# Loading the tokens by two queues, and taking the first norm's sums of squares from token-major tiles

## The chip, the cores and the metric

The kernel runs on one core of one Trainium2 chip. The core has five engines that run side by side, each in its own instruction order: TensorE (PE, with its weight loads shown apart as PEld), VectorE (DVE), ScalarE (ACT), GpSimd (POOL) and SyncE (SP). SP and ACT also issue DMA transfers; an issue is an instruction in their order like any other. The metric is the device time of one execution in microseconds (us). The kernel before takes 1518.39 us, the median of three runs (1518.27 to 1519.29).

## The reference

Two pre-norm residual layers over 512 tokens of width 1024, then a final RMSNorm. What matters for the change is the head of the first layer:

```
h = rms_norm(x, norm1_g[l])          # y = x * rsqrt(mean(x*x) + EPS); y * g
z = h @ w_in[l]
(u_ssm, dq, dk, dv, iq, ik, iw, rq, rk, rv, rg, gates) = split_cols(z)
ya = s5_mixer(u_ssm, ...)
yb = dsa_mixer(rope(dq), rope(dk), dv, rope(iq), rope(ik), iw)
yc = retention_mixer(rope(rq), rope(rk), rv, rg, ...)
x = x + (g_a*(ya @ w_proj_a) + g_b*(yb @ w_proj_b) + g_c*(yc @ w_proj_c)) @ w_out[l]
x = x + square(relu(rms_norm(x, norm2_g[l]) @ w_ff1[l])) @ w_ff2[l]
```

The factor rsqrt(mean(x*x) + EPS) is one number for each token. Scaling by it can be done after the product with w_in, and the kernel does so.

## The kernel before, in words

The tokens arrive token-major: eight tiles `xt` of 128 tokens x 512 channels (256 KB each), four token blocks t for each half hf of the channels. PE transposes them in groups of four into a PSUM bank `tr` of 128 channels x 512 tokens; there are eight such groups m. From each bank ACT writes `xgh` (the tokens times the gain g1, rounded to float32r), DVE writes the remainder `xgl`, DVE copies the bank to the residual page `x`, and ACT squares it (`sq`) while DVE adds the square to one page `ssq`. Each float32 product is made of three float32r products: high x high, high x low, low x high. A weight tile is loaded as `raw` by SP, cast to `wh` on ACT, and its remainder `wl` is made on DVE; three buffers of each go round.

`Norm.stats` turns `ssq` into one factor for each token. Four products with a column of ones (`stat`) sum over the partitions, DVE forms mean + EPS (`st_v`), POOL raises it to the power -0.5 (`st_r`), DVE puts the four blocks on diagonals (`sq<-ct,st_r`), PE spreads them over all partitions (`statb`), and ACT copies the result out (`rbc`).

After the tokens, layer 0 goes on with the product for keys, values and indexer (`mm`, 292 columns, `tm_group(l, C_DK, ...)`), whose four banks ACT moves out as `z<-mm,st_r`, scaled by `st_r`; with the product for the state-space branch (`mx`, two blocks of 512 tokens), which DVE scales by `rbc` into `s5u` and ACT and POOL shuffle in 32 small copies into `u`; and with the query product (`mm`, 384 columns, `C_DQ`). Its four PSUM banks are those of the 292-column product, so it starts when the first `z` is out. Then come products for gates (`mm`, 512 columns), which fill PE while DVE, ACT and POOL prepare the state-space and attention branches.

The order of each engine is not written by hand: a scheduler orders the instructions at build time from priorities (weight loads are taken early) and from its own model of the time. At run time each engine keeps its order and waits on semaphores. DMAs use eight semaphores in turn (DMAHW0 to DMAHW7); an issue also waits until the transfer that used its semaphore last has landed.

All calls go through one helper, so the profile puts nearly everything on line 110; instructions are told apart by the names of their tiles.

Of the kernel before, what the change touches and what calls it, by code (L numbers as in the profile page):

```python
# [12 lines left out]
AF = mybir.ActivationFunctionType  # L13
ALU = mybir.AluOpType

P = 128
SEQ = 512
DM = 1024
DEPTH = 2
KB = DM // P  # L20
NT = SEQ // P
EPS = 1e-6
# [71 lines left out]
def build(tc, x, positions, norm1_g, w_in, lam_re, lam_im, log_step, b_re, b_im, c_re, c_im, ssm_d,  # L94
# [5 lines left out]
    class Ordered:  # L100


        def __init__(self, e):
            self._e = e
# [16 lines left out]
    pe, ve, sc, gp, sy = (Ordered(e) for e in (nc.tensor, nc.vector, nc.scalar, nc.gpsimd, nc.sync))  # L121
    es = contextlib.ExitStack()
    with es:
# [4 lines left out]
        def f(t):  # L128
            return t.bitcast(F32)

        def page(dtype=F32, name="pg", tag="pg"):
            t = pool.tile([P, 512], dtype, tag=tag, bufs=BUFS[tag], name=name)
            pending[t.tensor.name] = tag
            return t

        def tpage(dtype=F32, name="ta"):
            return page(dtype, name, "ta")
# [7 lines left out]
        def small(n, name, bufs=2, dtype=F32):  # L145
            return pool.tile([P, n], dtype, tag=name, bufs=bufs, name=name)
# [4 lines left out]
        def mx_ps(name="mx"):  # L151
            return psp.tile([P, 512], F32, tag="mx", bufs=4, name=name)

        def copy(o, i, scale=1.0):
            sc.activation(o, i, AF.Copy, scale=scale)
# [4 lines left out]
        def stt(o, a, s, b, op0, op1):  # L160
            ve.scalar_tensor_tensor(o, a, s, b, op0=op0, op1=op1)

        ct = cp.tile([P, CONSTS.shape[1]], F32, name="ct")
        xt = {}
        rows = [spage(name="rows"), spage(name="rows")]
        with tc.high_priority():
            sc.dma_start(out=ct[:, :P], in_=consts[:, :P])
            sc.dma_start(out=rows[0][:DEPTH * KB, :P], in_=norm1_g.rearrange("l (k p) -> (l k) p", p=P))
            for hf in range(2):
                for t in range(NT):  # L170
                    z = tpage(name="xt")
                    sy.dma_start(out=z, in_=x[0, t * P:(t + 1) * P, hf * 512:(hf + 1) * 512])
                    xt[hf, t] = z

        def cst(n):
# [4 lines left out]
        ones = cp.tile([P, P], F32, name="ones")  # L180
# [10 lines left out]
        g1 = cp.tile([P, DEPTH * KB], F32, name="g1")  # L191
# [8 lines left out]
        def more_consts():  # L200
            z = rows[1]
            gp.memset(z[:, :P], 0.0)
            for name, src in (("g2", norm2_g.rearrange("l (k p) -> (l k) p", p=P)),
                              ("rg", ret_g.rearrange("l (k p) -> (l k) p", p=P)),
                              ("gb", glu_b.rearrange("l (k p) -> (l k) p", p=P)),
                              ("lr", lam_re.rearrange("l (i a) p -> (l i) (a p)", a=2)),
                              ("li", lam_im.rearrange("l (i a) p -> (l i) (a p)", a=2))):
                o, n = R_OFF[name], src.shape[0]
                sy.dma_start(out=z[o:o + n, :P], in_=src)
            o = R_OFF["sd"]  # L210
            sy.dma_start(out=z[o:o + 8 * DEPTH, 96:P], in_=ssm_d.rearrange("l (i a) c -> (l i) (a c)", a=2))
            q = z[96:96 + 8 * DEPTH]
            sy.dma_start(out=q[:, P:P + 2], in_=log_step.rearrange("l (i a) -> (l i) a", a=2))
            ve.tensor_copy(q[:, :P].rearrange("p (a s) -> p a s", s=64), q[:, P:P + 2, None].to_broadcast([8 * DEPTH, 2, 64]))
            ps = columns(z, 96 + 8 * DEPTH)
            ve.tensor_copy(vec[:, :N_ROWS], ps[:, :N_ROWS])
            ve.tensor_copy(vec[:, N_ROWS:], ps[:, 96:96 + 8 * DEPTH])
            glb2 = cp.tile([P, DEPTH * 2], F32, name="glb2")
            ve.tensor_scalar(glb2, vec[:, R_OFF["gb"]:R_OFF["gb"] + 2 * DEPTH], 0.5, None, op0=ALU.mult)
            sy.dma_start(out=ct[:, P:], in_=consts[:, P:])  # L220
            return glb2
# [68 lines left out]

        class Norm:
            def __init__(self):
                self.h, self.l, self.acc = [None] * KB, [None] * KB, None

            def feed(self, m, gcol, src=None, cc=slice(0, SEQ), room=None):
                src = xp[m][:, cc] if src is None else src
                if gcol is not None:
                    h, lo = (page(F32R, n, "xg") if room is None else room() for n in ("xgh", "xgl"))
                    copy(h, src, gcol)
                    stt(lo, src, gcol, f(h), ALU.mult, ALU.subtract)  # L300
                    self.h[m], self.l[m] = h, lo
                if self.acc is None:
                    self.acc = page(name="ssq", tag="ssq")
                if m == 0:
                    sc.activation(self.acc[:, cc], src, AF.Square)
                else:
                    s = page(name="sq", tag="sq")
                    sc.activation(s[:, cc], src, AF.Square)
                    ve.tensor_tensor(self.acc[:, cc], self.acc[:, cc], s[:, cc], ALU.add)

            def pair7(self, k, gc, ngc, room):
# [11 lines left out]
                for src, h, lo in ((t1, ah, al), (t2, ch, cl)):  # L323
# [4 lines left out]
                return [(z[:, q], y[:, q]) for z, y, q in ((oh, ol, ha), (eh, el, ha), (eh, el, hz), (ch, cl, hz),  # L328
                                                          (ah, al, ha), (ch, cl, ha), (ah, al, hz))]

            def stats(self, bc=True, ts=range(NT)):
                ps = mx_ps("stat")
                for t in ts:
                    pe.matmul(ps[:, 2 * t:2 * t + 2], self.acc[:, t * P:(t + 1) * P], ones[:, 0:2], start=True, stop=True)
                v = small(NT, "st_v")
                tt = slice(ts[0], ts[-1] + 1)
                ve.tensor_scalar(v[:, tt], ps[:, 0:2 * NT].rearrange("p (t a) -> p t a", a=2)[:, tt, 0], 1.0 / DM, EPS,
                                 op0=ALU.mult, op1=ALU.add)
                r = small(NT, "st_r")
                gp.tensor_tensor(r[:, tt], v[:, tt], nhalf[:, tt], ALU.pow)  # L340
                if not bc:
                    return r, None
                dg = page(name="sq", tag="sq")
                for t in range(NT):
                    ve.tensor_scalar(dg[:, t * P:(t + 1) * P], ident, r[:, t:t + 1], None, op0=ALU.mult)
                pb = mx_ps("statb")
                pe.matmul(pb, ones, dg, start=True, stop=True)
                rb = page(name="rbc", tag="rbc")
                copy(rb, pb)
                return r, rb  # L350
# [379 lines left out]
        def tr4(blocks, psf=None):  # L730

            ps = (psf or mx_ps)("tr")
            for t, b in enumerate(blocks):
                w = b.shape[-1]
                pe.transpose(ps[:w, t * P:(t + 1) * P], b, ident)
            return ps
# [514 lines left out]
        nrm = Norm()  # L1251
        for m in range(KB):
            if m == 4:
                glb2 = more_consts()
            ps = tr4([xt[m // 4, t][:, (m % 4) * P:(m % 4 + 1) * P] for t in range(NT)])
            nrm.feed(m, g1[:, m:m + 1], ps)
            xp[m] = page(name="x%d" % m)
            mark.append(ve.tensor_copy(xp[m], ps).ins.name)
        o5 = None
        for l in range(DEPTH):  # L1260
            nrm, o5 = layer(l, nrm, o5)
# [22 lines left out]
```

## Time and profile before

| what | value |
|---|---|
| median of three runs | 1518.39 us |
| the profiled execution | 1518.57 us, span 1516.8 us |
| PE, PEld busy | 97%, 85% of the span |
| DVE, ACT, POOL busy | 81%, 46%, 4% |
| DMA, mean | 95 GB/s |
| TensorE clock granted, by slices of 38 us | under 0.9 of full only in the second (38 to 76 us) |

The span is from the first to the last recorded instruction; the profiled execution is 1.8 us longer. A line of a timeline gives start, duration, engine, operation, tile written <- tiles read, shape, and in brackets how long the engine had been idle before it and what released it. Start to start, not the duration, is what a matmul costs in a row of matmuls, because they overlap.

### The profile page before, as it was taken

How to read it: one execution, taken by the hardware profiler on the slowest of the kernel's cores; microseconds unless marked ns; L12 is line 12 of the kernel's file. 1: busy time of each engine (PE TensorE's matmuls, PEld its weight loads, DVE VectorE, ACT ScalarE, POOL GpSimd, SP SyncE). 2: the span in 40 equal slices, each digit the busy share in tenths (PEclk: the TensorE clock that was granted, in tenths of full speed). 3: DMA queues.
4: the chain of work that ended last, by engine and by line, in shares of the span. 5: the costliest groups of instructions: out<-in, count | busy, mean ns of one | idle time of the engine just before them, and what ended most of it. 6: DMA issues, size and time to landing. Idle time of an engine off the chain costs nothing.

```text
span 1516.8 us, 22081 instructions
## 1 busy us (share of the span) xinstructions
PE 1468.6 (97%) x8202; PEld 1288.4 (85%) x8202; DVE 1224.0 (81%) x2618; ACT 696.2 (46%) x1154; POOL 59.3 (4%) x131
## 2 busy tenths in 40 slices
PE   5999999999998999999999999999999999999997
PEld 5888988877887998889888889988778888998887
DVE  7876899985899878987775769998568888777876
ACT  5654653453534443344455743344445434343343
POOL 0211100000010000100001100000000000000000
PEclk9899999999999999999999999999999999999999
DMA  6221222323322333233342223322143323333343
GB/s 221 77 81 42 81 70 73 94 70 101 108 63 91 111 98 99 83 108 95 119 130 76 84 57 94 94 70 84 56 153 90 95 93 98 111 98 102 94 126 111
DMA packets 138993, 144.17 MB, mean 95 GB/s; under 512 B 11835, under 2 KB 131461, under 8 KB 138885
## 3 DMA queue, kind: packets, MB, share of 16 engines
q1 hardware_dynamic: 138132, 141.63, 31.0%
q8 instruction: 64, 1.05, 0.3%
q10 hardware_dynamic: 752, 1.12, 0.2%
q14 instruction: 45, 0.36, 0.1%
HBM read 136.44 MB, written 6.29 MB: 94 GB/s over the span
## 4 chain that ended last, share of the span: by engine, by line
PE 83%; DVE 10%; ACT 4%; issue 2%; DMA 1%; POOL 0%; SPq 0%; POOLq 0%; DVEq 0%; ACTq 0%
PE mm L110 58%; PE f L110 17%; DVE wl L110 2%; ACT u L110 1%; PE mx L110 1%; PE pv L110 1%; PE sp L110 1%; PE ry L110 1%; PE tr L110 1%; DVE zr L110 1%; DVE ang L110 1%; PE pt L110 1%; ACT s5f L110 1%; DVE x L110 1%; PE s5y L110 1%
## 5 line engine op out<-in xcount | busy, mean ns | idle before, releaser
L110 ACT ACTIVATE wh<-raw 128x1024 fp32r<-128x1024 f32 (+4 forms) x318 | 310.4, 978 | 528.6 <-PE mm L110 287.7
L110 DVE TENSOR_TENSOR wl<-raw,wh 128x1024 fp32r<-128x1024 f32 (+4 forms) x318 | 355.2, 1118 | 120.0 <-ACT wh L110 116.7
L110 PE MATMUL f<-xc,wh 128*128 128x256 f32 x1344 | 242.8, 281 | 0.0
L110 PE MATMUL mm<-sql,wh 128*128 128x512 f32 (+1 forms) x544 | 207.2, 382 | 1.3 <-DVE sql L110 1.2
L110 PE MATMUL mm<-sqh,wh 128*128 128x512 f32 (+1 forms) x544 | 207.0, 382 | 1.3 <-DVE fft L110 1.1
L110 PE MATMUL mm<-sqh,wl 128*128 128x512 f32 (+1 forms) x544 | 206.1, 381 | 0.0
L110 PEld LDWEIGHTS f<-xc,wh 128*128 128x128 f32 x1344 | 205.4, 188 | 0.0
L110 PE MATMUL f<-xc,wl 128*128 128x256 f32 x644 | 174.6, 281 | 1.3 <-DVE wl L110 1.3
L110 PE MATMUL mm<-xgh,wh 128*128 128x512 f32 x384 | 152.3, 397 | 0.0
L110 PE MATMUL mm<-xgh,wl 128*128 128x512 f32 x384 | 152.1, 397 | 0.0
L110 PE MATMUL mm<-xgl,wh 128*128 128x512 f32 x384 | 151.9, 396 | 0.0
L110 DVE TENSOR_TENSOR raw<-raw 128x256 f32<-128x256 f32 (+1 forms) x336 | 107.3, 330 | 30.0 <-DMA raw<-in_w_ff_dram 27.8
L110 PEld LDWEIGHTS mm<-sql,wh 128*128 128x128 f32 x544 | 102.3, 188 | 21.6 <-DVE sql L110 1.9
L110 PEld LDWEIGHTS mm<-sqh,wh 128*128 128x128 f32 x544 | 102.2, 188 | 21.7 <-issue 1.5
L110 PEld LDWEIGHTS f<-xc,wl 128*128 128x128 f32 x644 | 118.7, 188 | 1.9 <-DVE wl L110 1.5
L110 PEld LDWEIGHTS mm<-sqh,wl 128*128 128x128 f32 x544 | 102.4, 188 | 21.0
L110 PE MATMUL mm<-wl,xgh 128*128 128x384 f32 (+1 forms) x320 | 107.5, 338 | 1.7 <-DVE wl L110 1.7
L110 PE MATMUL mm<-wh,xgh 128*128 128x384 f32 (+1 forms) x320 | 103.5, 340 | 4.6 <-ACT z L110 2.8
L110 PE MATMUL mm<-wh,xgl 128*128 128x384 f32 (+1 forms) x320 | 104.5, 338 | 0.0
L110 DVE TENSOR_TENSOR x<-x,mm 128x512 f32<-128x512 f32 (+1 forms) x136 | 88.3, 650 | 12.9 <-PE mm L110 12.6
L110 PEld LDWEIGHTS mm<-xgh,wl 128*128 128x128 f32 x384 | 72.3, 188 | 16.1
L110 PEld LDWEIGHTS mm<-xgl,wh 128*128 128x128 f32 x384 | 72.3, 188 | 15.5
(383 smaller groups left out, 2676.9 us busy)
## 6 DMA issues: line engine op xcount, KB each, us to landing
raw<-in_w_ff_dram SPq DMA_DIRECT2D x76, 512.0 KB, 3.5
raw<-in_w_ff_dram SPq DMA_DIRECT2D x112, 256.0 KB, 2.8
raw<-in_w_in_dram SPq DMA_DIRECT2D x52, 512.0 KB, 3.6
raw<-in_w_in_dram SPq DMA_DIRECT2D x32, 384.0 KB, 3.3
raw<-in_w_out_dram SPq DMA_DIRECT2D x16, 512.0 KB, 3.4
xd<-x SPq DMA_DIRECT2D x16, 256.0 KB, 2.2
x<-xd SPq DMA_DIRECT2D x16, 256.0 KB, 5.6
raw<-in_w_proj_c_dram SPq DMA_DIRECT2D x8, 384.0 KB, 3.2
```

What stands on the lines that cost most here:

```text
L110: r = fn(*a, **k)
```

## The change

Two edits. First, the four token tiles of the second half (hf = 1) are issued by ACT's queue and not by SP's. Second, in the first norm of layer 0 alone, the squares are no longer taken from the transposed banks and added up on DVE. A new function `token_sums` squares each token-major tile on ACT as it stands in SBUF, with the sum over its 512 channels as a by-product of the instruction (`accum_out`); a DVE addition of four columns joins the two halves. `stats` then skips the four `stat` products. The later norms are as before.

```diff
-                    sy.dma_start(out=z, in_=x[0, t * P:(t + 1) * P, hf * 512:(hf + 1) * 512])
+                    (sc if hf else sy).dma_start(out=z, in_=x[0, t * P:(t + 1) * P, hf * 512:(hf + 1) * 512])
...
-            def feed(self, m, gcol, src=None, cc=slice(0, SEQ), room=None):
+            def feed(self, m, gcol, src=None, cc=slice(0, SEQ), room=None, squares=True):
...
+                if not squares:
+                    return
...
+            def token_sums(self, xt):
+
+                q = small(2 * NT, "st_q", 1)
+                for (hf, t), z in xt.items():
+                    s = page(name="sq", tag="sq")
+                    sc.activation(s, z, AF.Square, accum_out=q[:, hf * NT + t:hf * NT + t + 1])
+                self.sums = small(NT, "st_s", 1)
+                ve.tensor_tensor(self.sums, q[:, :NT], q[:, NT:], ALU.add)
+
             def stats(self, bc=True, ts=range(NT)):
-                ps = mx_ps("stat")
-                for t in ts:
-                    pe.matmul(ps[:, 2 * t:2 * t + 2], self.acc[:, t * P:(t + 1) * P], ones[:, 0:2], start=True, stop=True)
                 v = small(NT, "st_v")
                 tt = slice(ts[0], ts[-1] + 1)
...
+                if self.sums is None:
+                    ps = mx_ps("stat")
+                    for t in ts:
+                        pe.matmul(ps[:, 2 * t:2 * t + 2], self.acc[:, t * P:(t + 1) * P], ones[:, 0:2], start=True, stop=True)
+                    sums = ps[:, 0:2 * NT].rearrange("p (t a) -> p t a", a=2)[:, tt, 0]
+                else:
+                    sums = self.sums[:, tt]
+                ve.tensor_scalar(v[:, tt], sums, 1.0 / DM, EPS, op0=ALU.mult, op1=ALU.add)
...
-            nrm.feed(m, g1[:, m:m + 1], ps)
+            nrm.feed(m, g1[:, m:m + 1], ps, squares=False)
...
+        nrm.token_sums(xt)
```

The scheduler orders the first layer's mixer anew; from its end on the orders of all engines are the same. On ACT at the head of the program, from the third weight cast on, stood before:

```order
L110 ACTIVATE wh<-raw 128x584 [waits DMAHW4_49]
L110 ACTIVATE xgh<-tr,g_89 128x512 [waits DVE_49,PE_49]
L110 ACTIVATE xgh<-tr,g_89 128x512 [waits PE_49] x2
L110 ACTIVATE ssq<-tr 128x512 [waits DVE_49]
L110 ACTIVATE xgh<-tr,g_89 128x512 [waits PE_49]
```

and stands now:

```order
L110 ACTIVATE wh<-raw 128x584 [waits DMAHW4_49]
L110 DMA xt<-in_x_dram 128x512 x2
L110 DMA xt<-in_x_dram 128x512 [waits DMAHW6_49]
L110 DMA xt<-in_x_dram 128x512 [waits DMAHW0_49]
L110 ACTIVATE sq,st_q<-xt 128x512 [waits DMAHW5_49]
L110 ACTIVATE sq,st_q<-xt 128x512
L110 ACTIVATE xgh<-tr,g_89 128x512 [waits DVE_49,PE_49]
L110 ACTIVATE sq,st_q<-xt 128x512 [waits DMAHW7_49,Activation_49]
L110 ACTIVATE sq,st_q<-xt 128x512 [waits DMAHW1_49,Activation_49]
L110 ACTIVATE xgh<-tr,g_89 128x512 [waits PE_49]
```

Four issues and two squares have come in front of the first `xgh`, and two more squares between the first and the second. The fourth issue waits for DMAHW0, the semaphore of the fourth `raw` tile.

On PE at the end of the 292-column product stood before (the last rows of that product, `stat`, and the first of the query product):

```order
L110 MATMUL mm<-wh,xgl 128x292 [waits DVE_49]
L110 MATMUL mm<-wh,xgl 128x292 x3
L110 MATMUL stat<-ones,ssq 128x2 [waits DVE_49,PE_49]
L110 MATMUL stat<-ones,ssq 128x2 x3
L110 MATMUL mm<-wh,xgh 128x384 [waits Activation_49]
L110 MATMUL mm<-wl,xgh 128x384
```

Now `statb` and the first products of the state-space branch stand inside the 292-column product, in its sixth and seventh groups of twelve:

```order
L110 MATMUL statb<-sq,ones 128x512 [waits DVE_49,PE_49]
L110 MATMUL mm<-wh,xgl 128x292 [waits DVE_49]
L110 MATMUL mm<-wh,xgl 128x292 x3
L110 MATMUL mm<-wh,xgh 128x292 [waits Activation_49]
L110 MATMUL mm<-wl,xgh 128x292
L110 MATMUL mm<-wh,xgh 128x292
L110 MATMUL mm<-wl,xgh 128x292
L110 MATMUL mm<-wh,xgh 128x292
L110 MATMUL mm<-wl,xgh 128x292
L110 MATMUL mm<-wh,xgh 128x292
L110 MATMUL mm<-wl,xgh 128x292
L110 MATMUL mx<-xgh,wh 128x512 [waits DVE_49,PE_49]
```

What moved: `stat` is gone, and the query product, which followed it, now comes after all 48 products `mx`, none of which waits for the factors.

On ACT after the shuffles of the state-space input (`u`, 24 of the 32 copies) stood before, up to the cast of the query product's fourth and last weight tile:

```order
L110 ACTIVATE u<-s5u 32x128 x11
L110 ACTIVATE kt<-tr 128x512 [waits PE_49] x2
L110 ACTIVATE vhl<-z_501 128x4x64
L110 ACTIVATE ikt<-tr 128x512 [waits PE_49]
L110 ACTIVATE iqs<-z_501 128x4x32 [waits DMAHW7_49]
L110 ACTIVATE iqs<-z_501 128x4x32 x3
L110 ACTIVATE iqs<-z_501 128x4x32 [waits DMAHW3_49]
L110 ACTIVATE iqs<-z_501 128x4x32
L110 ACTIVATE wh<-raw 128x768 [waits DMAHW4_49,PE_49]
```

and stands now:

```order
L110 ACTIVATE u<-s5u 32x128 x11
L110 ACTIVATE iks<-z_492 128x4x32 [waits DVE_49]
L110 ACTIVATE iks<-z_492 128x4x32
L110 ACTIVATE kt<-tr 128x512 [waits PE_49] x2
L110 ACTIVATE vhl<-z_492 128x4x64
L110 ACTIVATE wh<-raw 128x768 [waits DMAHW4_49,PE_49]
```

The cast has moved ahead of `ikt` and the six `iqs`.

## Rows read from the trace of the kernel before

**Rows 1.** Waits of PE, 0 to 100 us: total, times, longest.

```profile
PE stat L110 <- DVE ssq L110: 4.0, 1, 4.0
PE mm L110 <- ACT z L110: 2.8, 1, 2.8
PE mm L110 <- DVE wl L110: 1.7, 1, 1.7
PE mm L110 <- ACT wh L110: 1.6, 1, 1.6
```

**Rows 2.** Chain that ended last, 0 to 110 us: start, duration.

```profile
34.38 1.06 POOL st_r L110
...
68.36 16.90 PE mm L110 x65
```

**Rows 3.** Timeline of PE and its weight loads, 8 to 75 us.

```profile
11.43 0.72 PEld L110 LDWEIGHTS tr<-ct,xt 128*128 128x128 f32 x4 [0.41 <-DMA xt<-in_x_dram]
...
32.20 1.02 PE L110 MATMUL stat<-ones,ssq 128*128 128x2 f32 x8 [4.04 <-DVE ssq L110]
36.01 0.69 PE L110 MATMUL mm<-wh,xgh 128*128 128x384 f32 x1 [2.79 <-ACT z L110]
...
40.02 1.05 PE L110 MATMUL statb<-sq,ones 128*128 128x512 f32 x2
...
54.42 0.34 PE L110 MATMUL mm<-wh,xgh 128*128 128x384 f32 x1
54.60 0.34 PE L110 MATMUL mm<-wl,xgh 128*128 128x384 f32 x1
...
65.72 0.97 PE L110 MATMUL mm<-wh,xgh 128*128 128x384 f32 x4 [1.63 <-ACT wh L110]
...
70.12 0.52 PE L110 MATMUL mm<-wh,xgl 128*128 128x384 f32 x1
70.44 0.52 PE L110 MATMUL mm<-wl,xgh 128*128 128x384 f32 x1
```

**Rows 4.** Busy time in stretches: PE, PEld, DVE, ACT, POOL, granted clock, DMA share, GB/s.

```profile
10.00:15.00 5.00, 4.85 (x28) 4.05 (x27) 2.33 (x4) 3.06 (x6) 0.00 (x0) 1.00 1.02 345
...
35.00:40.00 5.00, 3.99 (x12) 3.99 (x13) 5.00 (x46) 2.74 (x8) 0.42 (x1) 0.50 0.00 1
...
65.00:70.00 5.00, 2.62 (x9) 2.30 (x10) 5.00 (x14) 2.56 (x3) 0.00 (x0) 0.74 0.11 14
70.00:75.00 5.00, 5.00 (x19) 4.96 (x18) 4.97 (x15) 1.94 (x4) 0.00 (x0) 0.58 0.88 275
```

**Rows 5.** The same view, longer stretches.

```profile
160.00:200.00 40.00, 36.30 (x210) 33.83 (x210) 34.53 (x102) 26.21 (x60) 3.49 (x11) 0.96 0.26 76
200.00:330.00 130.00, 130.00 (x651) 111.63 (x650) 125.41 (x311) 52.94 (x100) 4.67 (x4) 1.00 0.27 80
```

**Rows 6.** Timeline of ACT, 0 to 70 us.

```profile
0.73 0.44 ACTq L110 DMA_DIRECT2D ct<-in_consts_dram  x1
...
7.89 0.69 ACT L110 ACTIVATE wh<-raw 128x584 fp32r<-128x584 f32 x1 [2.03 <-DMA raw<-in_w_in_dram]
11.95 1.84 ACT L110 ACTIVATE xgh<-tr,g 128x512 fp32r<-128x512 f32 x3 [3.37 <-PE tr L110]
...
50.20 5.29 ACT L110 ACTIVATE u<-s5u 32x128 f32<-32x128 f32 x12 [2.90 <-DVE s5u L110]
...
64.84 2.72 ACT L110 ACTIVATE wh<-raw 128x768 fp32r<-128x768 f32 x3
```

**Rows 7.** Groups by form, ACT, 0 to 260 us: count, busy us, mean ns, idle before.

```profile
L110 ACT ACTIVATE sq<-tr 128x512 f32<-128x512 f32 x7 | 4.0, 608 | 1.8 <-DVE ssq L110 1.8
...
L110 ACT ACTIVATION_READ_ACCUMULATOR sm<-sm,at_nm 128x1 f32 x6 | 1.1, 187 | 0.0
```

**Rows 8.** Groups by form, DVE, 0 to 40 us.

```profile
L110 DVE TENSOR_TENSOR ssq<-ssq,sq 128x512 f32<-128x512 f32 x7 | 4.8, 681 | 0.0
```

**Rows 9.** Waits of DVE, 0 to 200 us.

```profile
DVE wl L110 <- ACT wh L110: 19.5, 10, 5.4
```

More of the change, by code (lines that the diff above doesn't have):

```diff
@@ L292, in __init__ @@
             def __init__(self):
-                self.h, self.l, self.acc = [None] * KB, [None] * KB, None
-            def feed(self, m, gcol, src=None, cc=slice(0, SEQ), room=None):
+                self.h, self.l, self.acc, self.sums = [None] * KB, [None] * KB, None, None
+            def feed(self, m, gcol, src=None, cc=slice(0, SEQ), room=None, squares=True):
                 src = xp[m][:, cc] if src is None else src
@@ L329, in pair7 @@
                                                           (ah, al, ha), (ch, cl, ha), (ah, al, hz))]
+            def token_sums(self, xt):
[5 more added lines that the diff above has]
+                ve.tensor_tensor(self.sums, q[:, :NT], q[:, NT:], ALU.add)
             def stats(self, bc=True, ts=range(NT)):
-                ps = mx_ps("stat")
-                for t in ts:
-                    pe.matmul(ps[:, 2 * t:2 * t + 2], self.acc[:, t * P:(t + 1) * P], ones[:, 0:2], start=True, stop=True)
                 v = small(NT, "st_v")
                 tt = slice(ts[0], ts[-1] + 1)
-                ve.tensor_scalar(v[:, tt], ps[:, 0:2 * NT].rearrange("p (t a) -> p t a", a=2)[:, tt, 0], 1.0 / DM, EPS,
-                                 op0=ALU.mult, op1=ALU.add)
+                if self.sums is None:
[6 more added lines that the diff above has]
+                ve.tensor_scalar(v[:, tt], sums, 1.0 / DM, EPS, op0=ALU.mult, op1=ALU.add)
                 r = small(NT, "st_r")
```

## The prediction

> **What bounds the kernel now.** I read the page first: PE is busy for nearly the whole span, so the question is where it is not, and what ends the wait there. The waits of PE over the first 100 us answer it [rows 1]. Four of them belong to the first norm and to what follows from it. PE waits 4.0 us for the page `ssq`, 2.8 us for `z`, and twice, 1.6 and 1.7 us, for the last weight tile of the query product. The reader is to see that the first two are one story: `ssq` is summed on DVE behind seven additions, the factors need one more step on POOL [rows 2], and only with them can ACT empty the banks that the query product wants. The timeline of PE [rows 3] and the busy times by stretches [rows 4] add the part that is easily missed. After each of the two stories the clock is granted at half (0.50 of full between 35 and 40 us, 0.58 between 70 and 75), so PE also runs slowly when it runs again. The chain of waits shows the third thing: from 68.36 us on it is PE itself [rows 2], so time that PE gains ahead of that point is not lost again at once.
>
> **What goes.** All of this is PE time, and PE's order is what the chain follows there.
> - The wait for `ssq`, 4.04 us, and the eight `stat` products, 1.02 us [rows 3]. The sums now come from tiles that are in SBUF long before; the last token tile's square stands ahead of the fourth weight cast on ACT.
> - The wait for `z`, 2.79 us [rows 3]. `z` needs only `st_r`, which is early now, and PE has the 48 products `mx` to do meanwhile.
> - Slow running after it: the twelve query products from 36.01 to 40.02 us take 4.01 us, 0.334 each; at full clock one starts 0.18 after the other (54.42, 54.60). That is 12 x 0.154 = 1.85 us.
> - The two waits for the fourth weight tile, 1.6 + 1.7 = 3.3 us [rows 1]. Its cast stands on ACT behind 24 shuffles (12 take 5.29 us), `kt`, `vhl`, `ikt` and `iqs`, and comes at 64.84 [rows 6]. In the new order `ikt` and `iqs` are behind it, PE has twelve more query products to do before it needs the tile (12 x 0.18 = 2.2 us), and the shuffles start as soon as the first `mx` block is out.
> - Slow running after these: 20 products at a spacing of 0.32 (70.12, 70.44) where 0.18 would do, 20 x 0.14 = 2.8 us.
>
> Sum: 4.04 + 1.02 + 2.79 + 1.85 + 3.3 + 2.8 = 15.8 us.
>
> The seven additions on DVE go too, 7 x 0.68 = 4.8 us [rows 8], but DVE is not what I follow here; that counts in a rival below. The squares themselves stay: eight before, eight now, 0.61 us each [rows 7].
>
> **What comes.**
> - ACT at the head. Four issues of about 0.44 us [rows 6] stand behind the third weight cast, which ends at 8.58. ACT idles there for 3.37 us before its first `xgh` [rows 6], so three of them are hidden. The fourth waits for the fourth `raw` tile. No row has that landing; it was issued just ahead of the fourth token tile on the same queue, and PE had that one at 11.43 [rows 3], so I take at most 11.4, and at least 10.5. Then come 0.44 and two squares. An accumulating activation is followed by a read of the accumulator, 0.19 us [rows 7], so a square costs 0.6 to 0.8. The first `xgh` starts between 12.2 and 13.4 where it was 11.95. Behind it stand the other `xgh`, so PE waits: a group of twelve products of 292 columns takes about 12 x 0.18 x 292/384 = 1.6 us, and two squares and an `xgh` take up to 2.3, twice. Bounds 0.3 and 2.9 us for all; I take 1.8, near the middle, since neither end has a nearer row.
> - The factors on DVE. The new order puts the diagonals ahead of the fifth remainder `xgl`, and they wait for POOL's 1.06 us [rows 2] and two hand-overs. PE waits for that `xgl`. Bounds: nothing, if DVE is late there anyway, and 2.0; I take 1.3.
> - What is left of the wait for the fourth weight tile: ACT must get through `z`, a table load, two casts and `ks` before the first shuffle, and this may be 1 to 2 us after the `mx` block is ready. Between nothing and all of it back (6.1 us with the slow running); I take 0.7.
> - Ten more gate products now stand ahead of the state-space step (`dr`), 10 x 0.18 x 512/384 = 2.4 us of PE. If the branch behind it sets the end of the mixer, that much of the gain does not arrive; PE stands idle for 3.7 us between 160 and 200 us already [rows 5]. Between 0 and 2.4; I take 1.0.
> - The moved transfers save SP four issues. SP waits for data and buffers there, not for its own issues, so I take nothing. The DMA engines are full between 10 and 15 us with SP's queue almost alone (share 1.02, 345 GB/s) [rows 4]; the same bytes take the same time.
>
> The page "DMA: Bandwidth & Descriptors" of the Trainium skill (section "Issuing engines are not separate DMA queues") speaks against the first edit: transfers started by different engines end up on the same 16 DMA engines, and a second issuing engine saves only the time of issuing. The full share in [rows 4] agrees. By that rule the edit is worth nothing of itself, as in the sum; if a second queue added bandwidth, the first `xgh` would not be late and the sum would be about 1.5 us better.
>
> Net: 15.8 - 1.8 - 1.3 - 0.7 - 1.0 = 11.0 us. From the profiled execution's own 1518.57 (span 1516.8 and 1.8 around it) that is 1507.6; the median of the runs is 0.2 lower, so 1507.4 us.
>
> **Rivals.**
> - *Only the first story ends.* The shuffles start late, or DVE makes the remainder of the fourth weights late; PE waits again and the clock drops again. The gain is 15.8 - 6.1 - 1.8 - 1.3 - 1.0 = 5.6, so 1512.8. For it: ACT is full there (two runs of 12 shuffles at 5.29 us each, with a cast between them [rows 6]). Against: the cast has moved forward in the order. Chance 0.18.
> - *DVE is the pace.* Up to 330 us DVE has little room (125.41 of 130 us busy from 200 on [rows 5]). If it sets the time all along, the gain is its 4.8 us of additions less the 1.3 for POOL: 1514.9. Against: before 200 us it waited 19.5 us for weight casts alone [rows 9], and such waits move with PE. Chance 0.09.
> - *Slower.* The same engine, with waits in its order that it did not have: the head's 1.8 us, POOL's 1.3, and the casts of the third and fourth query weights, which stand behind the shuffles on ACT. DVE has waited ten times for a cast, 1.95 us in the mean and 5.4 at the longest [rows 9]; one of each makes 7.4. That is 10.5 us against 4.8 saved: 1518.4 + 5.7 = 1524.1. It decides once DVE has idled over 4.8 us more than before by the time of the top-k near 190 us. Against: DVE's waits for casts so far come from ACT waiting for PE, and PE is earlier. Chance 0.05.
> - *The second queue adds bandwidth*, or the head costs nothing: 1518.4 - 12.5 = 1505.9; with all costs at their lower ends, 1518.4 - 15.5 = 1502.9. Chance 0.06.
> - That the sums are not earlier at all would need the last square after 30 us; eight tiles of 256 KB take 6.1 us at the 345 GB/s of [rows 4], and eight squares 6.4 us. I give it nothing.
>
> **How the numbers follow.** Forecast 0.62, with its own range 1503 to 1511; the rivals 0.18, 0.09, 0.05 and 0.06. The range 1502 to 1515 takes in the first rival and about half of the second, and leaves out the slow one. What a measurement of this kernel can tell from no change is about 0.2%, 3.0 us, so faster means under 1515.4. Faster: 0.62 + 0.06 + 0.18 and a little over a third of the second rival, 0.03, is 0.89; I take 0.88. Slower 0.05, and 0.07 for no difference.
>
> **What would show it.** In the profile after: no wait of PE of over 2 us between 20 and 60 us, the granted clock at 1.00 from 20 us on to beyond 80, the query product whole behind `mx`, its last weights cast 10 to 13 us before the 64.84 of now, and no wait of PE behind that cast of over 1 us. The head is right if the first `xgh` starts at 12 to 13.5. Wrong would be: a granted clock near 0.5 in any 5 us before 80 us (the first rival), DVE without idle time up to 120 us and PE waiting for remainders (the second), or a head in which PE's first 292-column product starts later than 14 us.

## The result and the profile after

The changed kernel takes 1497.88 us in the median of 4 runs (1496.56 to 1499.47), the kernel before 1518.33 in the same measurement; the ratio is 0.9866, with a 95% interval of 0.9849 to 0.9883. That is 20.5 us less, where the forecast said 11.0, and it lies below the range of 1502 to 1515. The profiled execution took 1497.72 us with a span of 1495.9, against 1518.57 and 1516.8 before.

The page of the changed kernel (busy time and share of each engine; then PE's busy tenths and granted clock in 40 slices):

```profile
PE 1450.0 (97%) x8194; PEld 1279.6 (86%) x8194; DVE 1219.5 (82%) x2612; ACT 697.5 (47%) x1162; POOL 68.8 (5%) x131
...
PE   7999999999999999999999999999999999999997
...
PEclk9999999999999999999999999999999999999999
```

PE is as full as before, in a span that is shorter by 20.9 us. The waits of PE over the first 100 us, to be held against [rows 1]:

```profile
PE cols L110 <- DMA rows<-in_norm_g_dram: 4.4, 1, 4.4
PE tr L110 <- DMA xt<-in_x_dram: 3.8, 1, 3.8
PE tr L110 <- DVE iks L110: 2.2, 1, 2.2
PE mm L110 <- DVE xgl L110: 1.0, 1, 1.0
PE mm L110 <- ACT xgh L110: 0.8, 1, 0.8
```

All four waits of [rows 1] are gone. The first two rows here stood before too (4.6 and 3.7 us); the other three are new and small. PE's timeline, against [rows 3]:

```profile
8.42 3.73 PE L110 MATMUL tr<-ct,xt 128*128 128x128 f32 x16 [3.79 <-DMA xt<-in_x_dram]
12.93 0.41 PE L110 MATMUL mm<-wh,xgh 128*128 128x292 f32 x1 [0.77 <-ACT xgh L110]
...
24.26 0.80 PE L110 MATMUL mm<-wh,xgl 128*128 128x292 f32 x4 [1.03 <-DVE xgl L110]
...
25.97 1.02 PE L110 MATMUL statb<-sq,ones 128*128 128x512 f32 x2
...
41.58 0.34 PE L110 MATMUL mm<-wh,xgh 128*128 128x384 f32 x1
41.76 0.34 PE L110 MATMUL mm<-wl,xgh 128*128 128x384 f32 x1
...
53.35 0.66 PE L110 MATMUL tr<-ct,iks 128*128 128x128 f32 x4 [2.17 <-DVE iks L110]
```

The norm's factors are broadcast (`statb`) at 25.97 us, 14 us earlier, and the query products start 0.18 us apart. The same stretches as in [rows 4] (PE, PEld, DVE, ACT, POOL, granted clock, DMA share, GB/s):

```profile
10.00:15.00 5.00, 4.18 (x24) 3.38 (x23) 1.64 (x3) 4.04 (x11) 0.00 (x0) 1.00 1.01 354
35.00:40.00 5.00, 5.00 (x24) 4.10 (x23) 4.10 (x27) 2.77 (x5) 0.00 (x0) 1.00 0.29 79
65.00:70.00 5.00, 5.00 (x23) 4.10 (x23) 5.00 (x19) 1.06 (x1) 3.09 (x2) 1.00 0.37 105
70.00:75.00 5.00, 5.00 (x28) 4.17 (x27) 5.00 (x21) 2.54 (x3) 3.43 (x4) 1.00 0.49 120
```

Where PE ran at 0.50 and 0.58 of the clock it is now busy throughout at 1.00. ACT's timeline, against [rows 6]:

```profile
7.56 0.69 ACT L110 ACTIVATE wh<-raw 128x584 fp32r<-128x584 f32 x1 [1.96 <-DMA raw<-in_w_in_dram]
7.56 3.35 ACTq L110 DMA_DIRECT2D xt<-in_x_dram  x4
...
12.21 0.67 ACT L110 ACTIVATE xgh<-tr,g 128x512 fp32r<-128x512 f32 x1
...
53.97 0.84 ACT L110 ACTIVATE wh<-raw 128x768 fp32r<-128x768 f32 x1
```

So far nearly all stands as forecast. What was not forecast is further on. The first `statb` of the norm behind the first mixer starts at 437.23 us instead of 447.95: 10.7 us gained, nearly the forecast's 11.0. From there on the engines' instructions stand in the same order in both programs, but for a few of the first feed-forward part that are swapped (PE's last at 495 us), and yet the gain grows steadily: 12.6 us at the next layer's `statb` (782.8 against 795.4), 17.2 at the last (1164.1 against 1181.3), 20.9 at the end. One row of each kernel shows the pace. In the second layer's feed-forward part ACT copies one `zw` from the banks in each of its 14 steps; the row gives their count, shortest, median and longest time in ns, and the first and last start. First the kernel before, then the changed one:

```profile
L110 ACT ACTIVATE zw<-f x14: 361/364/367, 1194.3 to 1468.3; 128x256 f32<-128x256 f32 x14
```

```profile
L110 ACT ACTIVATE zw<-f x14: 363/364/366, 1177.1 to 1448.6; 128x256 f32<-128x256 f32 x14
```

Thirteen steps took 274.0 us and now take 271.5: 21.08 us a step, and 20.88. PE is 100% busy at clock 1.00 there in both. The same products simply follow each other faster.

### The profile page after: what moved, and what is told of

Same layout as the page of the kernel before. It is cut to its first block, busy times and chain, and to the rows that moved or that the text cites. A ratio compares the mean times of both kernels' runs of the same rounds, so it can differ in the third digit from the quotient of the medians.

```text
span 1495.9 us, 22071 instructions
## 1 busy us (share of the span) xinstructions
PE 1450.0 (97%) x8194; PEld 1279.6 (86%) x8194; DVE 1219.5 (82%) x2612; ACT 697.5 (47%) x1162; POOL 68.8 (5%) x131
## 3 DMA queue, kind: packets, MB, share of 16 engines
q10 hardware_dynamic: 1328, 2.17, 0.4%
## 4 chain that ended last, share of the span: by engine, by line
PE 84%; DVE 8%; ACT 3%; DMA 2%; issue 2%; POOL 0%; SPq 0%; POOLq 0%; DVEq 0%; ACTq 0%
PE mm L110 59%; PE f L110 16%; DVE wl L110 2%; ACT u L110 1%; DMA raw<-in_w_in_dram 1%; PE pv L110 1%; PE mx L110 1%; PE sp L110 1%; DMA raw<-in_w_ff_dram 1%; PE ry L110 1%; PE s5y L110 1%; PE pt L110 1%; ACT wh L110 1%; PE tr L110 1%; DVE raw L110 1%
## 5 line engine op out<-in xcount | busy, mean ns | idle before, releaser
L110 PEld LDWEIGHTS mm<-xgh,wh 128*128 128x128 f32 x384 | 72.4, 189 | 14.8
```

The source lines that it names most:

```text
L110: r = fn(*a, **k)
```

## The experiments

The theory I began with (A): the two small new tiles, `st_q` and `st_s`, shift the weight tiles and all behind them in SBUF, and TensorE's spacing depends on where its operands lie. In the programs as built the allocator puts each tile at a multiple of 32 B, so the two add 64 B to the distance between the pages that PE streams (`sqh`, `sql`, `xgh`, `xgl`) and the weight tiles `wh` and `wl`. (The change also moves `ssq` to the end, a whole page of 2048 B.) The rival (B): something in the instruction streams, queues or semaphores. "Distance" below is the weight tile's start less that of `sqh`, modulo 256 B; it is read from the built programs, 128 before and 192 after.

**Four runs: the addresses alone, and each half of the change alone.** An unused tile sets bytes aside without an instruction. before_pad64 and after_pad64 add this line to the kernel before and to the changed one:

```
             def stats(self, bc=True, ts=range(NT)):
+                pool.tile([P, 16], F32, tag="pad", bufs=1, name="pad")
                 v = small(NT, "st_v")
```

only_sums takes the first edit out of the changed kernel, only_queue makes that edit alone in the kernel before. In only_sums the scheduler orders the first mixer in yet another way, so it differs from the changed kernel in more than the issues; in only_queue the orders of PE, DVE and POOL are those of before.

```
only_sums
-                    (sc if hf else sy).dma_start(out=z, in_=x[0, ...
+                    sy.dma_start(out=z, in_=x[0, ...
only_queue
-                    sy.dma_start(out=z, in_=x[0, ...
+                    (sc if hf else sy).dma_start(out=z, in_=x[0, ...
```

> The kernel before with one unused block of 64 B per partition set aside between two tiles, no instruction more or less: the weight tiles and all behind them move by the 64 B by which the change's two little tiles move them against the activations. Theory A (where the tiles lie in SBUF sets TensorE's pace; the change gained 10 of its 20 us so): two FFN stages on a row take 41.8 us as in the changed kernel instead of 42.2, and the whole about 1508 us. Theory B (something in the instruction streams, queues or semaphores gave it): 42.2 us, 1518 us. Head as before under both: first x7-stage milestones of layer 0's mixer not earlier by more than 1 us.

> The changed kernel with 64 B per partition set aside, no instruction more or less, so that the weight tiles lie against the activations' tiles at the distance that they had before, modulo 128 B. Theory A, if only that distance modulo 128 B counts: two FFN stages 42.2 us, the whole about 1508 us, and the first `stat` of the second norm still at 425 us. Theory B: 41.8 us and 1498 us. Other addresses count than the weight tiles': something between.

> The changed kernel with all eight token-major tiles on SP's queue again; the sums of squares as in the change. Theory A: addresses are the changed kernel's, so 1498 us within 1.5 us if the second queue is worth nothing. Rival (the second queue is worth about a microsecond at the head): 1499 to 1500 us, with the first query product later by as much. Theory B with the queues as cause: 1508 us.

> The kernel before with half of the token-major tiles issued by ACT; the sums of squares as before. Theory A: addresses are those of before, so 1518 us, within 1.5 us. Rival (the second queue shifts which queue serves the later weight tiles, and that gave the 10 us): 1508 us, with two FFN stages in 41.8 us.

before_pad64 takes 1505.67 us, a ratio of 0.9914 (0.9897 to 0.9930): 13 us for 64 unused bytes. Its `zw` row has the changed kernel's pace, 271.6 us for 13 steps:

```profile
L110 ACT ACTIVATE zw<-f x14: 363/365/367, 1188.9 to 1460.5; 128x256 f32<-128x256 f32 x14
```

That is theory A, and B falls. after_pad64 was expected to lose it again if only the distance modulo 128 B counted; it takes 1496.29 us (0.9838, 0.9819 to 0.9856), with a step of 20.84 us, so that part of my theory was wrong. only_sums takes 1497.41 (0.9849, 0.9831 to 0.9868), a step of 20.88. only_queue takes 1522.19 (1.0017, 1.0006 to 1.0027), a step of 21.07: the second queue by itself costs 1 to 4 us. Its profiled execution took 1525.16 us, the slowest of its twelve runs, so the rows show the loss at its largest. Its head, on PE:

```profile
7.66 2.82 PE L110 MATMUL tr<-ct,xt 128*128 128x128 f32 x12 [2.75 <-DMA xt<-in_x_dram]
13.43 1.12 PE L110 MATMUL tr<-ct,xt 128*128 128x128 f32 x4 [2.95 <-DMA xt<-in_x_dram]
14.69 0.61 PE L110 MATMUL mm<-wh,xgh 128*128 128x292 f32 x1
```

and the issues on ACT, and SP's of the fourth token tile of the first half:

```profile
4.24 2.29 ACT L110 ACTIVATE wh<-raw 128x584 fp32r<-128x584 f32 x3 [1.01 <-DMA raw<-in_w_in_dram]
5.85 6.23 ACTq L110 DMA_DIRECT2D xt<-in_x_dram  x4
...
6.17 0.47 SPq L110 DMA_DIRECT2D xt<-in_x_dram  x1
```

and only_sums for comparison, first SP's issue of the same tile and then PE:

```profile
6.11 0.47 SPq L110 DMA_DIRECT2D xt<-in_x_dram  x1
...
7.18 2.82 PE L110 MATMUL tr<-ct,xt 128*128 128x128 f32 x12 [2.12 <-DMA xt<-in_x_dram]
10.54 1.12 PE L110 MATMUL tr<-ct,xt 128*128 128x128 f32 x4 [0.53 <-DMA xt<-in_x_dram]
11.92 0.61 PE L110 MATMUL mm<-wh,xgh 128*128 128x292 f32 x1 [0.27 <-ACT xgh L110]
```

The sixteen transposes are those of the groups 0 to 3, so they read the first half alone, and the last four read its fourth token tile. SP issues that tile at the same time in both programs, 6.17 and 6.11 us, but the four transposes start at 13.43 instead of 10.54, after a wait of 2.95 us instead of 0.53. What differs is that ACT, between its weight casts, sends off tiles of the second half from 5.85 us on, which PE needs last. The loss is at the head, and it differs from execution to execution: in the changed kernel's own profile ACT issues only from 7.56 us on, and all sixteen transposes run through from 8.42; in after_pad64 and after_pad192 it issues from 6.00 and 6.17, and the four wait 2.67 and 2.71 us. That the transfers took DMA time from each other is the likely reason, but no row shows the share of one tile.

**Four runs: which tiles, and back again.** before_weights64 moves `raw`, `wh` and `wl` by 64 B and all behind them by 256; before_others64 moves only what lies behind; after_pad192 gives the changed kernel the old distance of 128; sums_pad64 is only_sums with 64 B more (distance 0).

```
before_weights64, sums_pad64: [P, 16]; after_pad192: [P, 48]
+                pool.tile([P, ..], F32, tag="pad", bufs=1, name="pad")
                 v = small(NT, "st_v")
before_weights64: [P, 48]; before_others64: [P, 16]
                 lo = pool.tile([P, 1024], F32R, tag="wl", bufs=3, name="wl")
+                pool.tile([P, ..], F32, tag="pad2", bufs=1, name="pad2")
```

> The kernel before, no instruction more or less, with the weight tiles (`raw`, `wh`, `wl`) 64 B further along each partition and all tiles behind them 256 B further. Theory A1 (the distance of the weight tiles from the activations' tiles, modulo 256 B, sets the spacing of the products; it was 128 B and is 192 B now): an FFN step 20.9 us instead of 21.08, the products of 512 columns 229 ns apart instead of 232, the whole about 1507 us. Rival (tiles behind the weights count: accumulators' readers, the stack of `xc`): 21.08 us and 1518 us.

> The kernel before, no instruction more or less, with the weight tiles where they were and all tiles behind them (`z0`, `qT`, `xc`, `zz` and others) 64 B further. Theory A1: products `mm` of 512 columns 232 ns apart as before, since `sqh` and `wh` haven't moved; only the `f` products, whose `xc` moved, can change: a step 21.04 us, the whole 1516 to 1519 us. Rival: 20.9 us and about 1507 us.

> The changed kernel, no instruction more or less, with the weight tiles 192 B further, so that their distance from the activations' tiles is again what it was in the kernel before, 128 B modulo 256 B. Theory A1: the evenly grown part of the gain goes: an FFN step 21.08 us, about 1508 us, with the head still 10.7 us earlier at the first `stat` of the second norm. Rival (not that distance, another property of the old addresses): 20.85 us and 1497 us.

> The changed kernel with all token-major tiles on SP's queue, and 64 B set aside so that the distance of the weight tiles from the activations' tiles is 0 modulo 256 B. Theory A1 with the second queue worth a loss: the fastest of all, 1494 to 1496 us, an FFN step 20.84 us. If the second queue is worth nothing: 1496 us, as after_pad64.

before_weights64 takes 1508.74 us (0.9929, 0.9917 to 0.9942), before_others64 1521.24 (1.0013, 1.0004 to 1.0022), 2 us over the kernel before where at most no change was expected: the gain is the weight tiles'. after_pad192, with every instruction of the change, takes 1512.06 (0.9946, 0.9934 to 0.9959), 4 us more than the 1508 expected: 12 of the 20 us are gone, and the step is that of before:

```profile
L110 ACT ACTIVATE zw<-f x14: 362/364/364, 1185.9 to 1459.9; 128x256 f32<-128x256 f32 x14
```

sums_pad64 takes 1490.95 (0.9812, 0.9799 to 0.9826), by the ratios 4 us under after_pad64 at the same distance, which again speaks against the second queue.

**Four runs: the sums at the old distance, the queue in another order, and the rule for the distance.** sums_pad192 is sums_pad64 with 192 B in place of 64, sums_pad32 with 32. alternate_pad64 lets ACT issue the odd token blocks of both halves, and sums_aligned puts every tile that PE streams at the weight tiles' offset; both are made on top of sums_pad64:

```
sums_pad192: [P, 48]; sums_pad32: [P, 8]; the others [P, 16]
+                pool.tile([P, ..], F32, tag="pad", bufs=1, name="pad")
                 v = small(NT, "st_v")
alternate_pad64
-                    sy.dma_start(out=z, in_=x[0, ...
+                    (sc if t % 2 else sy).dma_start(out=z, in_=x[0, ...
sums_aligned
+            pool.tile([P, 48], F32, tag="pad3", bufs=1, name="pad3")
             o.q = pool.tile([P, 3, SEQ], F32, tag="qT", bufs=1, name="qT")
...
+            pool.tile([P, 48], F32, tag="pad4", bufs=1, name="pad4")
             g2c, ng2 = vector("g2", l, KB), small(KB, "ng2")
```

> The changed kernel with all token-major tiles on SP's queue, and the weight tiles at the distance from the activations' tiles that they have in the kernel before (128 B modulo 256 B): the sums of squares alone, without what the addresses give. The prediction's working, which is for such an arrangement: 11 us less than before, 1507 to 1508 us. Theory Q (the second queue itself costs a few us): 3 to 4 us under after_pad192's 1512, so 1508 us as well. Rival (second queue worth nothing): 1512 us, as after_pad192.

> As sums_pad64, with ACT issuing the token-major tiles of the odd token blocks, of both halves, in place of the second half. Theory Q1 (in the change the second queue's tiles, needed last, take the engines' time from those needed first): here both queues carry tiles in the order in which they are needed, the first product at 12 us, 1491 us as sums_pad64. Theory Q2 (the issue itself, 3.35 us on ACT ahead of its casts, is what costs): the first product a microsecond later, 1493 to 1496 us.

> As sums_pad64, with two more unused blocks of 192 B, so that the weight tiles and all tiles that TensorE streams against them (`sqh`, `sql`, `xc`, the gates' and mixers' pages) start at 32 B modulo 256 B. Theory A1: the `f` products, whose `xc` lay 0, 64 or 128 B off, come closer as well: from 118.2 ns apart to 117, 28 stages of 84 products, some 2 us and more in the other stages: 1486 to 1490 us. Rival (only the distance of `sqh` and `sql` mattered, and that is 0 already): 1491 us.

> The changed kernel with all token-major tiles on SP's queue and the weight tiles 224 B (modulo 256 B) from the activations' tiles, starting at 0 modulo 64 B. Theory A1 with a cost that falls steadily from distance 128 (232 ns a product of 512 columns) over 192 (229) to 0 (227): 228 ns and 1493 us. Rival (a start at 0 modulo 64 B is what counts): below 227 ns, and under 1491 us.

sums_pad192 takes 1507.45 us (0.9919, 0.9905 to 0.9933). The sums alone, with the old addresses, save 12 us; with the second queue (after_pad192) 8. alternate_pad64 takes 1489.92 (0.9806, 0.9791 to 0.9822), the same as sums_pad64, with PE's first product at 12.31 us: when the tiles are issued in the order of need the second queue does no harm, and no measurable good. ACT's issues there:

```profile
4.23 0.35 ACTq L110 DMA_DIRECT2D xt<-in_x_dram  x1
...
5.04 0.34 ACTq L110 DMA_DIRECT2D xt<-in_x_dram  x1
```

These two are the second and fourth token tiles of the first half, so the fourth goes out at 5.04 us, ahead of all of the second half, and none of the sixteen transposes waits over 0.24 us once the first has started. That fits the reading above. I did not test the order of the tiles apart from the number that each queue carries.

The other two went against me. sums_aligned takes 1495.12 us (0.9837, 0.9824 to 0.9851), 4 more than sums_pad64. Its step is 20.98 us:

```profile
L110 ACT ACTIVATE zw<-f x14: 364/367/367, 1172.3 to 1445.0; 128x256 f32<-128x256 f32 x14
```

In it the products of 256 columns come 119.9 ns apart in the mean, where they came 118.4 apart in sums_pad64. sums_pad32, at distance 224, takes 1507.56 (0.9921, 0.9907 to 0.9934): as slow as 128, though nearer to 0. No steady rule.

**Four runs: the missing distances.** They are sums_pad64 with 96, 128, 160 and 224 B set aside, distances 32, 64, 96 and 160:

```
sums_pad96: [P, 24]; sums_pad128: [P, 32]; sums_pad160: [P, 40]; sums_pad224: [P, 56]
+                pool.tile([P, ..], F32, tag="pad", bufs=1, name="pad")
                 v = small(NT, "st_v")
```

> The changed kernel with all token-major tiles on SP's queue, weight tiles 32 B (modulo 256 B) behind the streamed tiles' start. Theory S (an odd multiple of 32 B between the two costs most, whatever its size): products of 512 columns 233 ns apart, 1506 to 1508 us. Theory N (the nearer to 0, modulo 256 B, the better; 224 B was slow for the `xc` that moved with it): 228 ns, 1491 to 1494 us.

> As sums_pad96, with the distance at 64 B. Theory S: an even multiple of 32 B, and the mirror of 192 B: 229 ns, 1494 to 1498 us. Theory N: 229 ns as well; the two differ on 32 and 224 B. Rival (the order counts, weights ahead or behind): away from 229 ns, up to 232 and 1507 us.

> As sums_pad96, with the distance at 96 B. Theory S: 233 ns, 1506 to 1508 us. Theory N: between 229 (64 B) and 232 (128 B): 231 ns and 1500 to 1504 us.

> As sums_pad96, with the distance at 160 B. Theory S: 233 ns, 1506 to 1508 us. Theory N: between 232 (128 B) and 229 (192 B): 231 ns and 1500 to 1504 us.

The times are 1506.41 us (0.9912, 0.9897 to 0.9927), 1509.45 (0.9931, 0.9905 to 0.9958), 1513.18 (0.9958, 0.9944 to 0.9973) and 1511.20 (0.9944, 0.9929 to 0.9959). All four are slow. With PE's starts of all runs sorted by the distance of the two operands, for products of 512 columns that follow each other without a wait (over 3,000 starts each):

| distance, B | 0 | 32 | 64 | 96 | 128 | 160 | 192 | 224 |
|---|---|---|---|---|---|---|---|---|
| mean from start to start, ns | 227.6 | 233.2 | 233.3 | 234.1 | 232.4 | 233.4 | 229.3 | 233.2 |

Five of the eight distances (all but 0, 128 and 192) rest on one program each, but for a few starts. Two of eight are fast, 0 and 192. My theory S was half right (all odd multiples of 32 B are slow) and theory N wrong; 64 and 128 are slow as well. It is the distance and not the offset of either: some 512-column products stream `xc` tiles that moved along with the weights, and at distance 192 they come 229.5 to 230.0 ns apart with the `xc` tile at any of seven offsets.

**Two runs: the 256-column products.** The ten pages of one pool, which hold ten of 27 `xc` tiles, are moved from distance 0 to 64 or 192, on top of alternate_pad64:

```
alternate_ta64: [P, 48], then [P, 16]; alternate_ta192: [P, 16], then [P, 48]
+        pool.tile([P, ..], F32, tag="pad5", bufs=1, name="pad5")
         rows = [spage(name="rows"), spage(name="rows")]
...
+        pool.tile([P, ..], F32, tag="pad6", bufs=1, name="pad6")
         mark = []
```

> As alternate_pad64, with 192 B set aside ahead of the first pages and 64 B behind the token-major tiles' pages, so that the ten of 27 `xc` tiles that lay 0 B (modulo 256 B) before the weight tiles lie 64 B before them; the other distances are as in alternate_pad64. If distance alone sets the spacing of 256-column products too: those of these tiles go from 119.5 to 116.2 ns, an FFN step from 20.84 to 20.74 us, the whole 2 to 3 us less, 1487 to 1488 us. Rival (their spacing is a matter of the row of tiles, not of one distance): 20.84 us and 1490 us.

> As alternate_ta64, with 64 B ahead of the first pages and 192 B behind, which puts these ten tiles 192 B before the weight tiles: 117.6 ns, an FFN step 20.78 us, the whole 1 to 2 us less than alternate_pad64, 1488 to 1489 us. Rival: 20.84 us and 1490 us.

The steps came out as the distances say, 20.77 us for alternate_ta64:

```profile
L110 ACT ACTIVATE zw<-f x14: 365/366/367, 1172.8 to 1442.8; 128x256 f32<-128x256 f32 x14
```

and 20.79 for alternate_ta192. The whole is 1488.67 us (0.9800, 0.9783 to 0.9818) and 1489.58 (0.9805, 0.9791 to 0.9818): a measurement can't tell these from alternate_pad64. All three beat the changed kernel's 0.9866 by 9 to 10 us.

## Why the prediction was wrong

**The step that failed.** "From the profiled execution's own 1518.57 (span 1516.8 and 1.8 around it) that is 1507.6." Taking the net from the whole assumes that everything behind the edited part keeps its time because its instructions keep their order. It did not: the tiles moved, and PE's spacing with them. The term that the sum lacked can be sized from the trace. Over the whole program 3,552 products have 512 columns, 768 have 384 and 2,544 have 256; their mean spacing, where they follow each other without a wait at full clock, went from 232.25 to 229.42, from 175.89 to 174.66 and from 118.23 to 117.59 ns. That is 10.1 + 0.9 + 1.6 = 12.6 us. The runs give the same: after_pad192 against the changed kernel, 0.9946 - 0.9866 of 1518 us, is 12.1, and before_pad64 and before_weights64 show 13 and 11 by themselves.

**The price of the moved transfers.** "The moved transfers save SP four issues ... so I take nothing." They cost 1 to 4 us in only_queue (2.6 by its ratio). Three pairs at equal distance give 2.6 us (the changed kernel against only_sums, not clear of noise), 3.9 (after_pad64 against sums_pad64) and 4.1 (after_pad192 against sums_pad192), but their first mixers are ordered differently too. I asked whether the same bytes take longer, and not which of them come first. The Trainium skill ("DMA: Bandwidth & Descriptors", section "Issuing engines are not separate DMA queues") says that transfers started by different engines run interleaved on the same 16 DMA engines, and that a second issuing engine saves issue time alone. The full DMA share, 1.01 between 10 and 15 us, agrees that there was no bandwidth to win. The loss is one of order: a tile that PE needs first came late.

**How far the sum held.** The change as made, at the old distance, is after_pad192: it saves 8 us (6 to 10), 3 under the 11.0 of the working. The sums alone save 12 (10 to 14), and sums_pad192's 1507.45 us lies next to the 1507.4 of the working, but partly by luck: that run has no issues on ACT, for which the working had charged.

That the changed kernel is 10.7 us ahead at the end of the first mixer is partly luck too. At `dr` it was 10.3 us ahead (110.35 instead of 120.68), and PE had done twelve more gate products by then (12 x 0.23 = 2.8 us), so 13.1 in all. From `dr` to the next norm's first `statb`, before and after:

```profile
120.68:447.95 327.27, 319.03 (x1574) 271.90 (x1574) 279.00 (x630) 153.75 (x290) 20.31 (x35) 0.98 0.26 78
```

```profile
110.35:437.23 326.88, 313.94 (x1562) 270.69 (x1562) 278.00 (x627) 153.51 (x289) 20.02 (x35) 0.98 0.26 77
...
PE mm L110 <- ACT wh L110: 2.7, 1, 2.7
```

PE stood idle for 8.2 us there before and stands idle for 12.9 now. More than half of the 4.7 us is a wait for a weight cast at 142 us that was not there before. The working took 1.0 for this branch, with 2.4 as its bound. By the spacings above, an estimate, the 900 products of 512 columns and 344 of 384 in this stretch gave about 3 us back, which hid over half of it. after_pad192 is 8.3 us ahead at its end (439.66) and sums_pad192 11.6 (436.34), but the three heads differ as well: the first product starts at 12.93, 14.07 and 12.19 us.

**Step by step, in the changed kernel:**
- The waits for `ssq` and `z` and the `stat` products are gone, as said.
- Half clock after them: gone in both places, as said. Further on it fell in places where it had not: 0.66 of full between 110 and 115 us, and again between 140 and 145, at the new wait.
- The fourth weight cast is at 53.97 us, 10.9 earlier (10 to 13 said), and PE has no wait behind it. In only_sums, where PE comes a microsecond earlier, 1.1 us of that wait return (`wl`) and the wait for `iks` goes.
- ACT at the head: the first `xgh` at 12.21 (12.2 to 13.4 said); PE waits 0.77 us for it, 1.8 was taken.
- Factors on DVE: PE waits 1.03 us for `xgl`, 1.3 was taken.
- What is left of the wait for the weights: 0.7 was taken; it came in another place, 2.17 us for `iks`, which stands behind the 24 shuffles on ACT. "No wait of PE of over 2 us between 20 and 60 us" failed by that.
- Together 3.97 us of waits against 3.8 taken.
- Ten gate products ahead of `dr`: there are twelve, and behind them the waits that are told above, 4.7 us against 1.0 taken.

Of the rivals, none happened. Clock and waits rule out the first; DVE's waits for casts in the first 200 us fell from [rows 9] to 10.7 us, against the second and the slow one; the extra bandwidth is ruled out by only_queue.

## What to carry to other kernels

Before a gain or a loss is put down to an edit, see whether the edit also moved tiles in SBUF: here 64 B between weights and streamed tiles were worth more than the edit, and an unused tile of the right size is a control that costs no instruction. When all engines' orders agree and a steady stretch still runs at another pace, count its period (one row with first and last start will do) and look at addresses. A transfer given to a second queue can go out earlier than it is needed, and here the tile that was needed first then came late: give each queue its tiles in the order of need.

## What the runs showed of the hardware

- TensorE's spacing of 512-column float32r products, each with its own weight load of 128 columns, depends on the distance between weight tile and streamed tile modulo 256 B: 227.6 ns at 0, 229.3 at 192, 232.4 to 234.1 at the other six multiples of 32 B.
- Products of 256 columns prefer other distances: with every streamed tile at 0 they come 119.9 ns apart, the slowest mix seen; at 192 it is 117.6, at 64 116.5. So the best distance for the one kind is not that for the other.
- Why these distances are slow was not shown. Nothing in the traces separates the weight load's reads from the stream's.
- What the profile shows of the matmul itself hides this: between 1210 and 1450 us the mean duration of a 512-column product reads 394 ns before and 390 to 393 after. The starts tell it.
- A token tile of 256 KB issued by SP at 6.17 us was read 2.9 us later than the same tile issued at 6.11 in another program, when ACT had begun to issue others at 5.85 (one execution each).
